# A hybrid decoder layer on one Trainium2 core: the down-projection's 22 blocks in seven products, with the weight sums made in DRAM

## The chip, the cores and the metric

The kernel runs on one core of one Trainium2 chip. A core has a matrix engine (TensorE, in the profile PE; its weight loads are PEld) that multiplies a 128 x 128 weight tile with up to 512 columns and adds into banks of PSUM, a vector engine (VectorE, DVE), an activation engine (ScalarE, ACT), GpSimd (POOL) and a queue engine (SyncE, SP) that issues DMAs. ACT and POOL issue DMAs too; a DMA that adds to its destination is issued by POOL here. The metric is device time in microseconds, the median of three runs.

## The reference

One layer on x of 1024 tokens by 1024 channels, in float32. Only its last part matters here:

```python
def conv_ffn(xn, w_up, conv_w, conv_b, w_down):
    u = xn @ w_up                                # 1024 -> 2 x 2816
    upad = jnp.pad(u, ((0, 0), (CONV_WIDTH - 1, 0), (0, 0)))
    c = conv_b
    for j in range(CONV_WIDTH):                  # causal, width 3
        c = c + upad[:, j:j + S] * conv_w[j]
    gate, val = jnp.split(c, 2, axis=-1)
    return (jax.nn.silu(gate) * val) @ w_down    # 2816 -> 1024
...
    x = x + conv_ffn(xn, w_up[l], conv_w[l], conv_b[l], w_down[l])
return rmsnorm(x, norm_final_w)
```

Ahead of it lie a norm, the input projection, two attentions, gates and a mixing projection with a residual sum.

## The kernel before

Everything lies with channels on the 128 partitions and tokens along the row. Each float32 operand is split in two parts that sum to it: a high part (a cast by ACT) and a low part (a subtraction by DVE). A product of two blocks is three matmuls: high by high, weight-high by activation-low, weight-low by activation-high. A matmul needs the weight tile and the activation tile in parts, so DVE and ACT prepare both while PE works.

**Up-projection** (`hidden`, from line 922; its matmuls are line 919). It runs over 22 pairs j of output blocks (gate j, value j). A pair is a 2 x 2 block product done with seven products in place of eight; sums of weights are made by POOL (`sum_pair`, lines 121 to 124), sums of the seven results by DVE (`recombine`, lines 478 to 485, reading PSUM). Seven products of four blocks are 84 matmuls of 512 columns. Then POOL multiplies with the norm factor (line 1063), ACT and DVE apply the convolution (lines 1072 to 1075), DVE multiplies gate and value (1056), and SP stores the hidden block h_j to DRAM (`hd`). `next_w` keeps one pair of weights ahead; the weights' loads (`raw`, `rv`) are in SP's queue.

**Down-projection** (`down`, from line 1078). Output blocks m = 0 to 7, token halves 0 and 1, 22 hidden blocks.

- The first N1 = 6 hidden blocks are multiplied plainly: 16 pieces of three blocks, each for both halves (line 1120), so 288 matmuls; each output tile is added into `x3`, the residual, by DVE (line 1147).
- The other 16 blocks form a 2 x 2 problem (left and right eight blocks, upper and lower four outputs) in seven products P1, P5, P6, P3, P7, P2, P4, each over 4 outputs m and 8 blocks: 24 matmuls per step (line 1169). Products that share terms go on adding in the same PSUM bank ("chains": banks "y" for P1, P6, P7, P4 and "d" for P5, P3, P2), and after each DVE adds the bank into one or two tiles of `x3` (line 1176). A stage's activations are sums of h blocks (`operand`, DVE lines 1034 to 1045) that are then split (`parts_h`, lines 838 and 839). A stage's weights are sums too: four tiles `S` in SBUF are loaded by SP, negated by ACT (line 108) and added to by POOL's DMA (`add_to`, line 91) between stages.
- Step by step the program calls `next_w`, the product, loads of later h blocks (`fetch`), two `prep` calls (one operand each), and the evictions owed from the step before.
- The convolution of the last pair is deferred into the first pieces (`DEFER`), its stores likewise (`STORE`).
- P4's last two outputs are done in two halves of 256 columns, so that the final norm of the first quarter (`last_norm`: column sums on PE, a power on POOL, a spread on PE, scaling by DVE and POOL, stores) overlaps the last matmuls.

The compiler's tile layer orders each engine's instructions from the program's order and its own estimates; `issue_after` puts an instruction behind a given one on the same engine.

## Time and profile before

| | |
|---|---|
| median of three runs | 1330.38 us (1330.3 to 1331.21) |
| the profiled execution | 1330.42 us, its span 1328.4 us |
| granted TensorE clock | 0.998 |
| matmuls in the span | 6264 |
| up-projection, first pair to last | about 674.9 to 1097.3 us of the span |
| down-projection, plain part (line 1120) | 1097.3 to 1162.6 us |
| down-projection, seven products (line 1169) | 1162.6 to 1318.8 us |
| final norm and stores after the last matmul | 1318.8 to 1328.4 us |

Times within the span are counted from its first instruction. A "busy" engine is one with an instruction under way; for PE the ends are modelled, so the pace is read from starts or from the chain of waits, not from the mean of one matmul (which overlaps the next).

### The profile page before, as it was taken

How to read it: one execution, taken by the hardware profiler on the slowest of the kernel's cores; microseconds unless marked ns; L12 is line 12 of the kernel's file. 1: busy time of each engine (PE TensorE's matmuls, PEld its weight loads, DVE VectorE, ACT ScalarE, POOL GpSimd, SP SyncE). 2: the span in 40 equal slices, each digit the busy share in tenths (PEclk: the TensorE clock that was granted, in tenths of full speed). 3: DMA queues.
4: the chain of work that ended last, by engine and by line, in shares of the span. 5: the costliest groups of instructions: out<-in, count | busy, mean ns of one | idle time of the engine just before them, and what ended most of it. 6: DMA issues, size and time to landing. Idle time of an engine off the chain costs nothing.

```text
span 1328.4 us, 17040 instructions
## 1 busy us (share of the span) xinstructions
PE 1315.8 (99%) x6264; PEld 1097.6 (83%) x6264; DVE 1049.4 (79%) x1431; ACT 614.7 (46%) x946; POOL 478.0 (36%) x364
## 2 busy tenths in 40 slices
PE   9999999999999999999999999999999999999997
PEld 7888888888888878888888888888888888888886
DVE  8846775289888976455669999999999997886654
ACT  9432232276667774333444443343434344345643
POOL 0446652001101015751435666665566631101111
PEclk9999999999999999999999999999999999999999
DMA  7334333966554236334422222122222228867532
GB/s 260 126 144 157 145 148 122 269 179 190 143 133 142 82 126 225 120 118 151 143 95 95 80 79 93 66 95 80 82 77 86 81 75 333 266 158 143 111 98 108
DMA packets 63234, 180.25 MB, mean 136 GB/s; under 512 B 6960, under 2 KB 16816, under 8 KB 63152
## 3 DMA queue, kind: packets, MB, share of 16 engines
q1 hardware_dynamic: 49120, 153.48, 35.1%
q0 software_dynamic: 2304, 8.39, 3.7%
q10 hardware_dynamic: 11728, 17.31, 3.6%
q8 instruction: 49, 0.80, 0.3%
q14 instruction: 33, 0.27, 0.1%
HBM read 130.39 MB, written 48.76 MB: 135 GB/s over the span
## 4 chain that ended last, share of the span: by engine, by line
PE 97%; ACT 1%; DVE 1%; DMA 0%; issue 0%; SPq 0%; POOLq 0%; POOL 0%; ACTq 0%
PE t L919 45%; PE y L1169 7%; PE d L1169 5%; PE g L177 4%; PE g L178 4%; PE g L179 4%; PE sc L177 3%; PE sc L179 3%; PE sc L178 3%; PE sc L651 3%; PE y L1120 2%; PE d L1120 2%; PE t L667 1%; PE t L770 1%; PE sc L739 1%; PE t L679 1%
## 5 line engine op out<-in xcount | busy, mean ns | idle before, releaser
L1063 POOL TENSOR_TENSOR us<-us,rstd 128x1024 f32<-128x1024 f32 x42 | 92.2, 2214 | 82.5 <-DVE us L484 47.6
L1072 ACT ACTIVATE c<-us,vecs 128x1024 f32<-128x1024 f32 x44 | 54.8, 1248 | 127.1 <-POOL us L1063 121.5
L137 DVE TENSOR_TENSOR sl<-sf,sh 128x1024 fp32r<-128x1024 f32 x62 | 89.3, 1441 | 12.8 <-ACT sh L135 12.8
L158 DVE TENSOR_TENSOR wl<-raw,wh 128x1024 fp32r<-128x1024 f32 (+1 forms) x49 | 68.0, 1389 | 35.5 <-ACT wh L156 25.9
L135 ACT CAST sh<-sf 128x1024 fp32r<-128x1024 f32 x62 | 64.6, 1044 | 62.1 <-PE t L919 44.0
L156 ACT CAST wh<-raw 128x1024 fp32r<-128x1024 f32 (+1 forms) x49 | 49.6, 1014 | 91.2 <-PE sc L178 33.4
L121 POOL TENSOR_TENSOR sf<-rv 128x512 f32<-128x512 f32 x30 | 50.4, 1679 | 99.5 <-DVE sl L137 59.0
L1169 PE MATMUL y<-h,wh 128*128 128x512 f32 (+1 forms) x288 | 80.8, 366 | 0.0
L1075 DVE SCALAR_TENSOR_TENSOR c<-us,vecs,c 128x1024 f32<-128x1024 f32 x44 | 78.5, 1817 | 0.0
L1074 DVE SCALAR_TENSOR_TENSOR c<-us,vecs,c 128x1024 f32<-128x1024 f32 x44 | 69.3, 1606 | 5.6 <-ACT c L1072 5.5
L123 POOL TENSOR_TENSOR sf<-raw,rv 128x512 f32<-128x512 f32 x30 | 56.7, 1890 | 46.6 <-DVE sl L137 46.6
L177 PE MATMUL g<-xh,wh 128*128 128x512 f32 x176 | 71.0, 404 | 1.5 <-ACT g L580 1.5
L178 PE MATMUL g<-xl,wh 128*128 128x512 f32 x176 | 70.3, 400 | 0.0
L179 PE MATMUL g<-xh,wl 128*128 128x512 f32 x176 | 70.2, 399 | 0.0
L1055 ACT ACTIVATE c<-c 128x1024 f32<-128x1024 f32 x22 | 23.4, 1063 | 83.4 <-DVE c L1075 83.4
L655 DVE CUSTOM_DVE_ANT_0 L<-sc,bias 128x128 f32<-128x128 f32 (+7 forms) x64 | 47.7, 752 | 17.0 <-PE sc L651 13.7
L634 POOL MEMSET aT<- 128x128 f32 x32 | 6.1, 204 | 151.8 <-PE t L680 98.0
L137 DVE TENSOR_TENSOR wl<-raw,wh 128x1024 fp32r<-128x1024 f32 (+1 forms) x32 | 59.7, 1864 | 0.1
L1169 PE MATMUL d<-h,wh 128*128 128x512 f32 x192 | 59.4, 390 | 0.0
L1169 PEld LDWEIGHTS y<-h,wh 128*128 128x128 f32 x288 | 52.1, 189 | 8.7
L122 POOL TENSOR_TENSOR sf<-sf,raw 128x512 f32<-128x512 f32 x31 | 58.2, 1878 | 2.2
L656 ACT ACTIVATE L<-L,sm 128x128 f32<-128x128 f32 (+7 forms) x64 | 49.6, 778 | 20.0 <-DVE sm L655 17.3
(411 smaller groups left out, 4255.4 us busy)
## 6 DMA issues: line engine op xcount, KB each, us to landing
u<-qd SPq DMA_DIRECT2D x72, 256.0 KB, 6.4
raw<-in_w_up SPq DMA_DIRECT2D x23, 512.0 KB, 3.5
raw<-in_w_in SPq DMA_DIRECT2D x22, 512.0 KB, 3.7
hd<-c SPq DMA_DIRECT2D x22, 512.0 KB, 2.6
rv<-in_w_up SPq DMA_DIRECT2D x21, 512.0 KB, 3.6
gr<-gd SPq DMA_DIRECT2D x16, 512.0 KB, 3.4
S<-in_w_down POOLq DMA_DIRECT2D x16, 512.0 KB, 6.7
qd<-us SPq DMA_DIRECT2D x15, 512.0 KB, 2.6
```

Source lines behind the costliest of these rows:

```text
L122: tt(sa[:, 1], sa[:, 0], g[:, 0], ALU.subtract)
L135: cast = nc.scalar.copy(hi, src)
L137: low = nc.vector.tensor_tensor(lo, src, hi.bitcast(F32), ALU.subtract)
L158: self.lo = (eng or nc.vector).tensor_tensor(wl, raw, wh.bitcast(F32), ALU.subtract)
L177: nc.tensor.matmul(ps, wh[:, kc + o, :], ah, start=first and n == 0, stop=False)
L178: nc.tensor.matmul(ps, wh[:, kc + o, :], al, start=False, stop=False)
L179: nc.tensor.matmul(ps, wl[:, kc + o, :], ah, start=False, stop=last and n == len(kcs) - 1)
L919: nc.tensor.matmul(ps, (ah, ah, al)[p][:, k, :], (bh, bl, bh)[p], start=first and n == p == 0, stop=last and p == 2 and n == len(ks) - 1, ...
L1063: i = (nc.vector if m % NF == 0 else nc.gpsimd).tensor_tensor(us[:, 2:], us[:, 2:], self.rstd, ALU.mult)
L1074: nc.vector.scalar_tensor_tensor(c, us[:, 1:T + 1], cw[1], c, ALU.mult, ALU.add)
L1075: nc.vector.scalar_tensor_tensor(c, us[:, 0:T], cw[0], c, ALU.mult, ALU.add)
L1169: nc.tensor.matmul(ps, v[:, k, :], x, start=start and k == i == 0, stop=k == 7 and i == 2, skip_group_check=True)
```

## The change

All 22 hidden blocks go into the seven products (11 left, 11 right), and the plain part is gone. Each stage is cut in two steps per output, over blocks 0 to 5 and 6 to 10 (`CUTS`), so 18 and 15 matmuls a step. The order is P1, P2, P5, P6, P3, P7, P4. Signs move to the activations and evictions (`operand`, `evict`), so the weight sums are additions alone. They are made in DRAM tensors `sd` by `sums_of`: 16 copies issued by SP and 16 adding DMAs issued by POOL, each 128 rows of 1408 floats (704 KB), two steps per pair from pair 1 of the up-projection on, behind that pair's last weight load on SP (`self.sync`) and last weight sum on POOL (`self.sum`). The weights are then loaded like any other. The `S` tiles, their negation and additions in the down-projection go. P4 is split in columns only in its second cut. The scaling pieces of the first quarter are called among those of the last one, DVE's behind its last eviction.

```diff
-HP, HPB, HR = 11, 9, 8
-STORE = (1,9)
-DEFER = (4,8)
-N1 = 6
+HP, HPB, HR = 6, 14, 11
+STORE = (1, 6)
+DEFER = (2, 5)
+HK = NF // 2
+CUTS = ((0, 6), (6, 11))
-STAGES = ("P1", "P5", "P6", "P3", "P7", "P2", "P4")
+STAGES = ("P1", "P2", "P5", "P6", "P3", "P7", "P4")
...
-        if self.deep and self.wsrc and len(self.wsrc[0]) == 2 and not isinstance(self.wsrc[0][1], str):
-            src, nk = self.wsrc[0]
-            self.wsrc[0] = src, nk, None, None, self.load_raw(src, nk)
+        for i in range(min(2, len(self.wsrc)) if self.deep else 0):
+            if len(self.wsrc[i]) == 2:
+                self.wsrc[i] += None, None, self.load_raw(*self.wsrc[i])
...
+    def sums_of(self):
+        nc, d = self.nc, self.sd
+        row = lambda m, r: self.w_dn[m].rearrange("p k c -> p (k c)")[:, r * HK * P:(r + 1) * HK * P]
+        copy = lambda n, src: lambda m: nc.sync.dma_start(d[n][m], src(m))
+        add = lambda n, o, r: lambda m: nc.gpsimd.dma_start(d[n][m], row(m + o, r), accum_op=ALU.add)
+        for step in (copy("P5", lambda m: row(m + 4, 0)), copy("P7", lambda m: row(m + 4, 0)), add("P5", 4, 1), add("P7", 0, 0),
+                     copy("P6", lambda m: d["P5"][m]), add("P6", 0, 0), copy("P3", lambda m: d["P6"][m]), add("P3", 0, 1)):
+            for m in range(4):
+                step(m)
+                yield
...
+                    for _ in range(2 if j else 0):
+                        with tc.issue_after(self.sync), tc.issue_after(self.sum):
+                            next(sums, None)
...
         elif stage == "P6":
-            tt(a, a, R["B22", k], ALU.subtract)
+            self.nc.vector.scalar_tensor_tensor(a, a, -1.0, R["B22", k], ALU.mult, ALU.subtract)
...
-            def product(ps, w, stage, start, a=0, b=H2, each=None):
-                for k in range(8):
+            def product(ps, w, stage, c, start, a=0, b=H2, each=None):
+                k0, k1 = CUTS[c]
+                for k in range(k0, k1):
...
+            count = {0: 3, 1: 2, 3: 1, 6: 3, 7: 2}
+            chains, owed, tail, i = [{}, {}], [], [], 0
+            for stage in STAGES:
+                which, start, o, hf, done = plan[stage]
+                for c in range(2):
+                    for m in range(4):
+                        if stage == "P4" and c == 1 and m > 1:
+                            break
...
+                        product(ps, w, stage, c, start)
...
+                        prep(count.get(i, 0) if i < 8 else 2 if i % 4 < 2 or i < 16 else 1)
...
+                        if c:
+                            owed = [lambda ps=ps, m=m + o, hf=hf, done=done: evict(ps, m, hf, done)]
...
+                        i += 1
...
-                    product(ps, w, "P4", False, a, b, lambda k, m=m: tail.pop(0)() if a and k == (4 if m < 3 else 2) else None)
+                    product(ps, w, "P4", 1, False, a, b, each)
...
+                if a:
+                    def held(f):
+                        with tc.issue_after(ev.ins):
+                            f()
+                    last[1:1] = [lambda f=f: held(f) for f in tail[2:]]
+                    last[:0] = [lambda f=f: held(f) for f in tail[:2]]
```

## The prediction

> **What bounds the kernel now.** I read the page first, then the chain of waits in order of time, then the windows.

> ```profile
> PE 1315.8 (99%) x6264; PEld 1097.6 (83%) x6264; DVE 1049.4 (79%) x1431; ACT 614.7 (46%) x946; POOL 478.0 (36%) x364
> DVE  8846775289888976455669999999999997886654
> PEclk9999999999999999999999999999999999999999
> ```
> ```profile
> 702.10 395.23 PE t L919 x1740
> 1097.32 2.04 PE d L1120 x9
> ...
> 1160.56 2.04 PE y L1120 x9
> 1162.60 21.76 PE y L1169 x96
> ...
> 1316.95 1.80 PE y L1169 x15
> ```
> ```profile
> 930.00:968.00 38.00, 38.00 (x169) 31.23 (x168) 37.72 (x33) 15.64 (x18) 23.95 (x16) 1.00 0.25 84
> 1140.00:1160.00 20.00, 20.00 (x90) 16.57 (x89) 17.44 (x26) 7.30 (x13) 2.84 (x3) 1.00 0.83 254
> ...
> sum 200.00, PE 200.00 PEld 165.86 DVE 144.44 ACT 95.47 POOL 24.50; mean PE 20.00 PEld 16.59 DVE 14.44 ACT 9.55 POOL 2.45
> ```

> PE is busy 99%, at the full granted clock, and from 702.10 to 1318.76 the chain is matmul after matmul. The pace is 21.76 / 96 = 0.2267 us for a matmul of 512 columns (2.04 / 9 in the plain part, the same) and 1.80 / 15 = 0.12 us for one of 256. So a matmul that goes away in the down-projection is worth its pace, as long as the other engines keep up.

> The window rows (after the stretch: its length, then busy PE, PEld, DVE, ACT, POOL) are of different stages. The first, 38 us of the up-projection, has DVE at 37.72: there, DVE has no room either. The last sums ten windows of 20 us from 1100 to 1300, the down-projection, the middle row its fullest one: DVE 144 of 200, POOL 24.5. The change puts less on PE in the roomy stage, and new work on POOL and the DMA engines in the tight one.

> **The matmuls.** Before, counted from the code: 288 plain ones, and 7 x 4 x 24 = 672, of which P4's last two outputs (48) run as 96 of 256 columns. That is 912 full and 96 half. After: 7 x 4 x 33 = 924, of which the second cut of P4's last two outputs (2 x 15) runs as 60 halves: 894 full and 60 half. Gone are 18 x 0.2267 = 4.08 and 36 x 0.12 = 4.32, together **8.4 us**. Nothing hides this: the chain runs through these matmuls.

> **DVE, ACT and PSUM in the down-projection.**

> ```profile
> L158 DVE TENSOR_TENSOR wl<-S,wh 128x1024 fp32r<-128x1024 f32 x16 | 19.6, 1224 | 2.1 <-ACT wh L156 2.1
> L158 DVE TENSOR_TENSOR wl<-raw,wh 128x768 fp32r<-128x768 f32 x7 | 6.7, 956 | 3.3 <-ACT wh L156 3.2
> L839 DVE TENSOR_TENSOR h<-ha,h 128x512 fp32r<-128x512 f32 x32 | 20.8, 689 | 2.1 <-ACT h L838 2.1
> L1041 DVE TENSOR_TENSOR hb<-hc,hb 128x512 f32<-128x512 f32 x8 | 5.8, 733 | 1.7 <-DMA hc<-hd 1.6
> L1147 DVE TENSOR_TENSOR x<-x,d 128x512 f32<-128x512 f32 x8 | 5.5, 683 | 0.0
> L156 ACT CAST wh<-raw 128x768 fp32r<-128x768 f32 x7 | 5.8, 828 | 9.7 <-PE y L1120 7.3 <-issue 2.4
> ```

> Weight tiles: 8 x 0.956 + 28 x 1.224 = 41.9 before. After, 28 of six blocks (0.956) and 28 of five (no row; between 0.956 for six and 0.689 for four, I take 0.82) are 49.7: +7.8. Operand splits go from 62 to 71: 9 x 0.689 = +6.2. Operand sums go from 32 to 44: 12 x 0.69 to 0.73, +8.5 (the fused form that replaces some is an estimate at the same length). Evictions lose the plain part's 16: -10.9. DVE gains 11.6 us and stands near 156 of some 192 us, 81%. The average leaves room; the bursts are what to look at.

> With a step number i (eight per stage), the program puts eight operands into steps 12 to 15, all of stage P5's with a sum: 8 x 1.38 = 11.0, weights 3 x 0.82 + 0.96 = 3.4, three evictions with norms 4.1: 18.5 us against 60 matmuls, 13.6 us. Steps 8 to 11 before it have 12.0 us against 72 x 0.2267 = 16.3. Together 30.5 against 29.9. Two things ease it: these operands are first needed at step 16, and DVE's instructions overlap:

> ```profile
> 1147.84 2.50 DVE L839 TENSOR_TENSOR h<-ha,h 128x512 fp32r<-128x512 f32 x4
> ```

> Four in 2.50 is 0.62 each, a tenth under the mean of one, which makes 27.5 of 29.9. What would hurt PE is a weight tile split late. A tile's buffer comes free a step ahead, so in a step of 15 matmuls (3.40 us), after the cast (0.828 at most) and the split (0.82), DVE may be 1.75 us late. I take 0.6 us for the whole stage; the bounds are 0 (it runs ahead in steps 8 to 11) and 3.5, worked out under the rivals. ACT had 95 of 200 and loses the negations; POOL loses the adds here. The new operands wait for h loads as the old ones do, and PSUM is no tighter: one chain set of four banks starts where the plain part filled eight at once.

> **The sums in DRAM, on SP, POOL and the DMA engines.**

> ```profile
> L91 POOL DMA_DIRECT2D S<-in_w_down x16: 856/866/1105, 1153.8 to 1247.5; - x16
> S<-in_w_down POOLq DMA_DIRECT2D x16, 512.0 KB, 6.7
> q0 software_dynamic: 2304, 8.39, 3.7%
> q1 hardware_dynamic: 49120, 153.48, 35.1%
> 1153.83 1.98 POOL L91 DMA_DIRECT2D S<-in_w_down  x2 [17.04 <-DMA S<-in_w_down]
> rv<-in_w_up SPq DMA_DIRECT2D x21, 512.0 KB, 3.6
> ```
> ```profile
> 951.48 0.68 DVE L480 TENSOR_TENSOR u<-t,s 128x512 f32<-128x512 f32 x1
> 952.25 0.45 PE L919 MATMUL t<-T_0h,sh 128*128 128x512 f32 x1
> 952.54 0.39 PE L919 MATMUL t<-T_0l,sh 128*128 128x512 f32 x1
> 953.91 0.10 POOL L1062 MEMSET us<- 128x2 f32 x1
> 956.09 4.40 POOL L1063 TENSOR_TENSOR us<-us,rstd 128x1024 f32<-128x1024 f32 x2 [2.08 <-DVE us L484]
> 956.51 2.12 DVE L137 TENSOR_TENSOR wl<-rv,wh 128x512 fp32r<-128x512 f32 x1
> 960.52 1.25 ACT L1072 ACTIVATE c<-us,vecs 128x1024 f32<-128x1024 f32 x1 [1.15 <-POOL us L1063]
> 961.49 2.47 DVE L1074 SCALAR_TENSOR_TENSOR c<-us,vecs,c 128x1024 f32<-128x1024 f32 x2
> ```
> ```profile
> POOL sf L123 <- DVE sl L137: 39.8, 18, 2.3
> POOL us L1063 <- DVE us L484: 37.4, 18, 2.1
> POOL sf L121 <- DMA rv<-in_w_up: 36.7, 17, 3.4
> PEld t L919 <- DVE u L480: 1.6, 7, 0.2
> ```

> Thirty-two steps, two per pair from pair 1, end at pair 16. Pairs 1 to 4, 9, 10, 13 and 14 have copies alone, issued by SP behind that pair's loads. Each add or copy that needs an earlier step needs one issued four to six pairs ago, so no engine waits there. Eight pairs (5 to 8, 11, 12, 15, 16) have two adds each on POOL.

> An add behind POOL's last sum falls into the gap of 2.08 us before line 1063, where POOL waits for DVE. The old adds held POOL for 0.866 us; they have 128 rows too, longer ones now. Two are 1.73 us: inside the gap. If the issue grew with the bytes (704 / 512), two would be 2.4, and line 1063 would start 0.3 late. Behind it wait ACT's two convolutions, then DVE; the second ends at 961.77, and DVE's second instruction on line 1074 begins near 962.7 (half of 2.47 on), so about 1 us more is free. Past that, DVE is late, and PE with it: PE's weight load waits for line 480 in 7 of 18 pairs, because that frees the bank of the next product (it ended at 952.16; PE's matmul of 952.25 took 0.45, the next one 0.39). The up-projection has a pair in 84 x 395.23 / 1740 = 19.08 us, against 19.04 from the pace: a microsecond that DVE loses there stays lost, and the most that a lucky shift could win over all pairs is 22 x 0.04 = 0.8.

> The adds' transfers: 3.7% of 1328 us over 16 is 3.07 us of all engines per 512 KB, so 4.2 per 704 KB, two in a pair of 19.1 us are 0.44 on top of the window's 0.25. There is room on average. The load `rv` would land later beside them; POOL's next sums wait for it, and behind them POOL waits 2.2 us for DVE anyway (line 123), so that much is free.

> [...]

> I take +0.3 us for the up-projection, with bounds -0.8 and +23.

> **The tail.**

> ```profile
> 1317.44 1.84 POOL L1259 TENSOR_TENSOR x<-x,rstd 128x768 f32<-128x768 f32 x1 [2.21 <-ACT rstd L1251]
> 1318.78 0.43 DVE x L1223
> 1320.88 0.70 POOL rs L194
> ```

> From the last matmul (1318.76) to the end are 9.6 us. The last two halves now hold 30 matmuls of 0.12 instead of 48, so the first quarter's scaling (POOL 1.84) no longer ends inside them: it begins about as the last matmul ends, holds POOL near the 2.1 us at which the last power wants it, and its stores crowd those of the last quarter. I take +0.4, bounds -0.3 and +1.8 (all of the 1.84).

> **Sum.** -8.4 + 0.6 + 0.3 + 0.4 = -7.1 us. The profiled execution took 1330.42 (its span of 1328.4 and 2.0 around it, which I leave as they are); the median of the runs is 1330.38, so nothing is corrected. **Forecast 1323.3 us.** With all low bounds 1330.4 - 8.4 - 0.8 - 0.3 = 1320.9.

> **Rivals.**

> *The bursts starve PE.* If operands don't run ahead, steps 12 to 15 are 18.5 - 13.6 - 1.75 = 3.1 us late, and stage P3's second cut (six operands of 1.38, 3.4, 4.1: 15.8 against 13.6) 0.4 more. That is 2.9 more than I took: 1326.2. For it: DVE is at 17.4 of 20 already in places of this stage. Against: PE never waited there, and loads of h run steps ahead.

> [...]

> *More than forecast.* POOL and DVE disturb each other: `wl<-rv` took 2.12 against 0.69 for the same form in the down-projection, while line 1063 ran. If line 1063 comes a little later, DVE may go first; PE's pace caps that at 0.8 us: 1321.

> [...]

> **How the numbers follow.** The forecast with its terms moved within their bounds (1321 to 1325.5) has 0.66; the bursts (to 1328) 0.14; the adds 0.16, of which the mild half of a third ends near no change; more than forecast 0.04. About 0.2% (2.7 us) is what a measurement can tell from none. Faster than 1327.7: 0.66 + 0.04 + most of the bursts and a little of the adds, 0.78; within: 0.08; slower: 0.14. The range 1320.4 to 1332 leaves out the bad end of the adds and little else; the likeliest case alone is 1321 to 1325.5.

> **What would show it.** Line 1169's matmuls: 924 in place of 960 by pace, and none of line 1120. In the chain, whether matmuls still follow one another after the up-projection, with gaps at steps 12 to 17 if bursts bite. In the up-projection, POOL's issue of one add against 0.87, and the pair's length against 19.08 in pairs 5 to 8: this decides between forecast and slower. The time from the last matmul to the end against 9.6. I am wrong if a pair with adds takes over 20 us, or if PE waits for weights over 3 us in all.

## The result, and the profile after

The changed kernel is slower: 1336.09 us median of 6 runs (1334.9 to 1337.98) against 1330.62 for the kernel before on the same chip (6 runs, 1330.3 to 1331.21), a ratio of 1.0041, 95% interval 1.0028 to 1.0054. The profiled execution took 1335.52 us, its span 1333.7. Forecast were 1323.3 and a range of 1320.4 to 1332.

The page of the changed kernel, busy time and instructions by engine:

```profile
PE 1312.1 (98%) x6210; PEld 1090.0 (82%) x6210; DVE 1056.9 (79%) x1456; ACT 621.2 (47%) x967; POOL 479.5 (36%) x364
```

The matmuls are gone as counted: 6264 before, 6210 after, 54 fewer, where 288 + 672 + 48 became 924 + 30. So the work left, and the time did not. PE's timeline says where it stayed; a bracket is idle time just before a row, and what ended it.

```profile
1097.88 0.62 PE L1112 MATMUL y<-sh,wh 128*128 128x512 f32 x2
...
1103.41 0.73 PE L1112 MATMUL y<-sh,wh 128*128 128x512 f32 x2 [1.30 <-ACT wh L139]
1105.48 0.51 PE L1112 MATMUL y<-sh,wl 128*128 128x512 f32 x1 [1.34 <-DVE wl L141]
...
1109.02 0.39 PE L1112 MATMUL y<-sl,wl 128*128 128x512 f32 x1
1112.02 0.73 PE L1112 MATMUL y<-sh,wh 128*128 128x512 f32 x2 [2.61 <-ACT wh L139]
...
1132.27 0.61 PE L1112 MATMUL y<-h,wh 128*128 128x512 f32 x2
1135.62 0.80 PE L1112 MATMUL y<-h,wl 128*128 128x512 f32 x1 [2.74 <-DVE wl L141]
1136.21 1.06 PE L1112 MATMUL y<-h,wh 128*128 128x512 f32 x2
...
1140.90 0.73 PE L1112 MATMUL d<-h,wh 128*128 128x512 f32 x2 [0.24 <-ACT wh L139]
```

Every one of these waits is for the cast (`wh`) or the split (`wl`) of a weight tile, and all lie in the first 43 us of the down-projection. After 1140.90 the timeline has no bracket until the tail. The waits of the stretch from 1095 to 1145 (total, times, longest):

```profile
PEld y L1112 <- DVE wl L141: 7.0, 5, 3.2
...
PE y L1112 <- DVE wl L141: 4.8, 4, 2.7
...
PE y L1112 <- ACT wh L139: 3.9, 2, 2.6
```

The difference can be laid out by the starts of matmuls. "Up" is from the up-projection's first `t<-T_0h,wl` to the first matmul of the down-projection, "down" from there to the start of the last one, "idle" the brackets of PE in "down".

| profiled execution | up | down | idle | time |
|---|---|---|---|---|
| before | 403.80 | 221.30 | 0 | 1330.42 |
| after | 404.62 | 225.69 | 9.00 | 1335.52 |

Down should have been 221.3 - 8.4 = 212.9. It is 12.8 us more, of which 9.0 are gaps. The other 3.8 are what follows a gap: two matmuls of 1136.21 took 0.86 to the next row, 0.43 each in place of 0.2267, and this pace held from 1135.62 to 1138.35; after the shorter gaps one matmul took 0.34. Up is 0.8 longer, and from the last matmul's start to the span's end it is 10.1 after 9.9 before. -8.4 + 12.8 + 0.8 + 0.2 = +5.4, and the spans differ by 5.3.

**What makes the tiles late.** First four rows of the kernel before, from the timelines of ACT, DVE and PE:

```profile
1102.28 0.81 ACT L156 CAST wh<-raw 128x768 fp32r<-128x768 f32 x1
...
1104.20 0.95 DVE L158 TENSOR_TENSOR wl<-raw,wh 128x768 fp32r<-128x768 f32 x1
...
1105.32 0.62 PE L1120 MATMUL d<-sh,wh 128*128 128x512 f32 x2
1105.78 0.39 PE L1120 MATMUL d<-sh,wl 128*128 128x512 f32 x1
```

This is the second weight tile. PE came to it at 1105.32. Its split ended at 1105.15, and the first matmul that takes the split (`wl`) began at 1105.78, 0.63 us later. So the tile was just as late before; nobody saw it, because the first one lasted 36 matmuls, both halves of the columns, 8.16 us from 1097.16. In the changed kernel the second tile:

```profile
1101.40 1.24 ACT L1056 ACTIVATE c<-us,vecs 128x1024 f32<-128x1024 f32 x1 [3.26 <-POOL us L1047]
1102.55 0.81 ACT L139 CAST wh<-raw 128x768 fp32r<-128x768 f32 x1
...
1104.47 0.95 DVE L141 TENSOR_TENSOR wl<-raw,wh 128x768 fp32r<-128x768 f32 x1
```

Cast and split end within 0.3 us of where they did before. But a tile now serves one half, 18 matmuls, 4.08 us, and PE wants it at 1101.96. In front of the cast stands a deferred convolution that waits 3.26 us for POOL. The next tiles follow from the chain of waits of the changed kernel (start, length, what):

```profile
1104.56 0.88 DVE wl L141
...
1105.45 0.34 SPq L129
...
1107.74 6.41 DMA ha<-hd
...
1114.17 0.04 ACT h L820
...
1114.70 0.84 ACT wh L139
...
1115.56 0.97 DVE wl L141
...
1116.60 2.01 POOL us L1047
...
1118.63 1.25 ACT c L1056
...
1119.91 0.06 DVE c L1058
...
1121.11 0.83 DVE wl L141
...
1121.98 2.86 PE y L1112 x12
```

Read it as a queue: the late split of the second tile (1104.56) frees the buffer for which the next weight load (L129) waits on SP, the loads of `h` stand behind that load, one of them takes 6.41 us to land, ACT's cast of that operand waits for it, the weight's cast stands behind that in ACT's order, its split behind it, POOL's multiplication for a convolution behind the split, the convolution behind POOL, the next split behind the convolution, and PE at the end. Before, this chain was matmul after matmul here, and the first loads of `h` for the later operands went out 7.4 us earlier. First the kernel before, then the changed one:

```profile
1098.46 1.44 SPq L1012 DMA_DIRECT2D hb<-hd  x3
```
```profile
1105.85 2.32 SPq L999 DMA_DIRECT2D ha<-hd  x5
```

The longest gap, 2.74 us at 1135.62, lies after the chain shown. The cast of that tile had ended at 1131.00, but its split began 3.75 us later, behind an operand's sum that waited for a load of `h`, an eviction and a convolution in DVE's order:

```profile
1131.65 1.39 DVE L1020 TENSOR_TENSOR ha<-ha,hb 128x512 f32<-128x512 f32 x2 [4.62 <-DMA hb<-hd]
...
1134.75 0.82 DVE L141 TENSOR_TENSOR wl<-raw,wh 128x640 fp32r<-128x640 f32 x1
```

### The profile page after: what moved, and what is told of

Read it like the earlier page. It is cut to its first block, busy times and chain, and to the rows that moved or that the text cites. A ratio compares the mean times of both kernels' runs of the same rounds, so it can differ in the third digit from the quotient of the medians.

```text
span 1333.7 us, 17123 instructions
## 1 busy us (share of the span) xinstructions
PE 1312.1 (98%) x6210; PEld 1090.0 (82%) x6210; DVE 1056.9 (79%) x1456; ACT 621.2 (47%) x967; POOL 479.5 (36%) x364
## 3 DMA queue, kind: packets, MB, share of 16 engines
q0 software_dynamic: 2304, 11.54, 4.5%
## 4 chain that ended last, share of the span: by engine, by line
PE 82%; DVE 7%; issue 4%; DMA 2%; POOL 2%; ACT 2%; SPq 0%; POOLq 0%; DVEq 0%; ACTq 0%
PE t L901 32%; PE y L1112 7%; PE d L1112 7%; PE g L160 4%; PE g L161 4%; PE g L162 4%; PE sc L161 3%; PE sc L162 3%; PE sc L160 3%; PE sc L633 3%; DVE wl L120 1%; DVE c L1058 1%; PE t L649 1%; DVE c L1059 1%; PE t L752 1%
## 5 line engine op out<-in xcount | busy, mean ns | idle before, releaser
L141 DVE TENSOR_TENSOR wl<-raw,wh 128x1024 fp32r<-128x1024 f32 (+2 forms) x85 | 97.3, 1145 | 52.7 <-ACT wh L139 43.0
L139 ACT CAST wh<-raw 128x1024 fp32r<-128x1024 f32 (+2 forms) x85 | 74.1, 873 | 130.2 <-PE y L1112 53.5
L120 DVE TENSOR_TENSOR sl<-sf,sh 128x1024 fp32r<-128x1024 f32 x62 | 95.9, 1548 | 14.7 <-ACT sh L118 14.7
L177 POOL TENSOR_TENSOR rs<-ms,mhalf 128x8 f32<-128x8 f32 (+2 forms) x9 | 13.3, 1474 | 235.8 <-DVE ms L175 229.7
L1112 PE MATMUL y<-h,wh 128*128 128x512 f32 (+1 forms) x324 | 96.1, 380 | 0.0
L1112 PE MATMUL d<-h,wh 128*128 128x512 f32 x264 | 81.3, 389 | 0.2 <-ACT wh L139 0.2
L1059 DVE SCALAR_TENSOR_TENSOR c<-us,vecs,c 128x1024 f32<-128x1024 f32 x44 | 74.4, 1724 | 0.0
L1112 PEld LDWEIGHTS y<-h,wh 128*128 128x128 f32 x324 | 60.1, 190 | 11.3
L1058 DVE SCALAR_TENSOR_TENSOR c<-us,vecs,c 128x1024 f32<-128x1024 f32 x44 | 64.3, 1490 | 4.1 <-ACT c L1056 3.9
L1112 PE MATMUL y<-h,wl 128*128 128x512 f32 (+1 forms) x162 | 61.9, 382 | 3.3 <-DVE wl L141 3.2
L120 DVE TENSOR_TENSOR wl<-raw,wh 128x1024 fp32r<-128x1024 f32 (+1 forms) x32 | 62.8, 1962 | 0.1
L638 ACT ACTIVATE L<-L,sm 128x128 f32<-128x128 f32 (+7 forms) x64 | 49.6, 778 | 19.9 <-DVE sm L637 17.3
## 6 DMA issues: line engine op xcount, KB each, us to landing
raw<-in_w_up SPq DMA_DIRECT2D x23, 512.0 KB, 4.9
raw<-in_w_in SPq DMA_DIRECT2D x22, 512.0 KB, 3.8
hd<-c SPq DMA_DIRECT2D x22, 512.0 KB, 2.6
rv<-in_w_up SPq DMA_DIRECT2D x21, 512.0 KB, 4.6
gr<-gd SPq DMA_DIRECT2D x16, 512.0 KB, 3.4
```

What stands on the lines that cost most here:

```text
L120: low = nc.vector.tensor_tensor(lo, src, hi.bitcast(F32), ALU.subtract)
L139: self.hi = nc.scalar.copy(wh, raw)
L141: self.lo = (eng or nc.vector).tensor_tensor(wl, raw, wh.bitcast(F32), ALU.subtract)
L1058: nc.vector.scalar_tensor_tensor(c, us[:, 1:T + 1], cw[1], c, ALU.mult, ALU.add)
L1059: nc.vector.scalar_tensor_tensor(c, us[:, 0:T], cw[0], c, ALU.mult, ALU.add)
L1112: nc.tensor.matmul(ps, v[:, k - k0, :], x, start=start and k == i == 0, stop=k == HK - 1 and i == 2, skip_group_check=True)
```

## The experiments

The theories have letters in the expectations. Q: the short tiles lost the cover that hid late casts and splits, which stand in ACT's and DVE's queues behind convolutions and operands that wait for POOL or for loads. A: the additions in DRAM cause it. D: the DMA engines are too full there, whatever the order. U: two additions in one pair lengthen the up-projection. Where one run is given, its time has no interval, and the changed kernel's own runs spread over 3 us; the traces carry those comparisons.

**Loads of h first** (an order of SP alone):

```diff
+            with tc.high_priority(300):
+                for n in range(2):
+                    fetch(*loads[n][0])
             for stage in STAGES:
...
-                        if i < 2:
-                            fetch(*loads[i][0])
```

> Only SP's order changes: the five loads of hidden blocks 6 to 10 are issued ahead of the fifth weight load, which waits for a buffer. Theory Q (weight tiles that now last 4.1 or 3.4 us sit in ACT's and DVE's queues behind instructions that wait for something else): the loads land about 5 us earlier, ACT no longer holds the third tile's cast behind their casts, PE's gap of 2.61 + 0.26 us near 1112 goes and with it some slow restart: 3 to 4 us less than the changed kernel, 1332 to 1333; the gaps near 1103, 1105 and 1135 stay. Theory D (the DMA engines are too crowded there, the loads land late whatever their order): nothing changes, about 1336.

Measured: 1335.69 us in one run; down 223.31, idle 7.99, up 406.72. The gap of 2.61 us at the third tile shrank to 1.22, as the `h` casts no longer waited so long (0.82 us at the longest for the first ones, 5.78 in the changed kernel), but gaps of 1.69 and 1.33 at the second tile and of 2.58 at 1135.77 stayed. The expected gain of 3 to 4 us did not come: down is 2.4 us shorter, up 2.1 longer. Late loads are one of the things ahead of the weights, not all of them.

**No deferred convolutions.** The last three convolutions, with their products and so rows 20 and 21 of `h`, are left out.

> The three deferred convolutions of the last pairs are left out (the blocks are stored as they come from the up-projection), everything else stays. Theory Q: POOL's multiplication and ACT's convolution no longer stand ahead of the weight casts, so the gaps of 1.30, 1.34 and 0.51 us near 1103, 1105 and 1122 go: 3 to 5 us less than the changed kernel, 1331 to 1333, while the gap near 1112 (late loads) stays. Theory D: under 1 us of change.

```diff
-                        self.defer.append(f)
+                        self.defer.append(lambda after=None, j=j, w=w, us=us: self.late.append(lambda: nc.sync.dma_start(self.hd[j], us[w][:, 2:])) if w else None)
```

Measured: 1330.68 in one run; down 219.15, idle 3.39. PE's longest gaps in the timeline of this kernel:

```profile
1105.04 0.50 PE L1112 MATMUL y<-sh,wl 128*128 128x512 f32 x1 [0.59 <-DVE wl L141]
...
1110.38 0.73 PE L1112 MATMUL y<-sh,wh 128*128 128x512 f32 x2 [1.42 <-ACT wh L139]
```

With the convolutions out, 5.6 of 9.0 us of gaps went, and down fell by 6.5. The gap at 1135 is gone altogether. The edit also takes work off ACT, DVE and POOL, so this run alone does not tell the order of the work from its amount.

**The kernel before with short tiles.** Nothing of the change but its tile size: the plain part's eight weight tiles of six blocks become sixteen of three, each for 18 matmuls.

```diff
-        src += [(self.w_dn[m:m + 2, :, n * c:n * c + n, :].rearrange("m p k c -> p m k c"), 2 * n) for m, c in self.pieces[::2]]
+        src += [(self.w_dn[m, :, n * c:n * c + n, :], n) for m, c in self.pieces]
```

> The kernel before, with the plain part's weights loaded and split in 16 tiles of three blocks in place of 8 of six: a tile lasts 18 matmuls, 4.1 us, as in the changed kernel, with the same bytes and the same matmuls. Theory Q: PE waits for weights in the first 25 us of the down-projection, 2 to 6 us in all, 1332 to 1337. Theory D, and the theory that the adds did it: no gaps, 1330.4 within 1 us.

Measured: 1340.87 in one run, 9.8 us over the kernel before beside it (1331.05); down 230.57 for 221.30, idle 5.45. Its timeline:

```profile
1103.15 0.73 PE L1118 MATMUL d<-sh,wh 128*128 128x512 f32 x2 [1.05 <-ACT wh L156]
1104.55 0.50 PE L1118 MATMUL d<-sh,wl 128*128 128x512 f32 x1 [0.66 <-DVE wl L158]
...
1117.93 0.73 PE L1118 MATMUL d<-h,wh 128*128 128x512 f32 x2 [1.29 <-ACT wh L156]
...
1130.32 0.50 PE L1118 MATMUL d<-h,wl 128*128 128x512 f32 x1 [2.45 <-DVE wl L158]
```

Gaps of the same kind in the same stretch, with neither new products nor sums in DRAM. Here 9.3 us are lost, 5.45 of them in gaps. So shorter tiles are enough to uncover the lateness, which is the core of Q. They do it in more than one way, and this run does not part them: the first gap lies at a cast about as late as before (1102.61 after 1102.28), the one at 1117.93 behind casts of `h` whose loads SP issued only at 1104.91, as in the changed kernel behind a weight load that waits for a buffer, and the one at 1130.32 behind a deferred convolution in DVE's order.

**No sums.** Copies and additions are left out, and the four stages that use sums read plain quarters of the weight.

> The copies and adds in DRAM are left out and the stages take plain quarters of the weights; all else stays. The up-projection should win back its 0.7 us. Theory Q and theory D: the gaps of the first 45 us of the down-projection stay, 1335 within 1. Theory A (the adds delay the up-projection's end, and the lateness is carried into the down-projection): gaps go too, 1324 within 2.

```diff
-                    for _ in range(2 if j else 0):
-                        with tc.issue_after(self.sync), tc.issue_after(self.sum):
-                            next(sums, None)
```

Measured: 1336.53 in one run, half a microsecond over the expected range; up 403.90, down 226.35, idle 6.73, with gaps of 1.73, 1.33 and 2.86 us where the changed kernel has them. Without the additions up is 0.7 us shorter than in the changed kernel's trace, and the down-projection loses as much; A falls.

**Another order at the border**, same arithmetic: the loads of `h` first, as above; the first two weight tiles ahead of the last convolution in the up-projection; POOL's multiplications apart from their convolutions, and early; in steps 0 to 15 everything else of a step behind its weight's cast and split.

```diff
...
+                        hi, lo = self.whi, self.wlo
+                        with ExitStack() as edges:
+                            if i < 16:
+                                edges.enter_context(tc.issue_after(hi.ins))
+                                edges.enter_context(tc.issue_after(lo.ins))
+                            if i in DEFER:
+                                self.defer.pop(0)(lo)
+                            prep(count.get(i, 0) if i < 8 else 2 if i % 4 < 2 else 1)
+                        if i in (0, 1):
+                            self.mults.pop(0)(lo)
...
```

> The changed kernel with the same arithmetic, and another order of the work around the start of its down-projection: the first two weight tiles are cast and split before the last deferred convolution's ScalarE part, the multiplications of the deferred convolutions run on GpSimd early, convolutions and operands of steps 0 to 15 are placed behind that step's weight cast and split, five loads of h go to SP ahead of the weights. Theory Q (a weight tile now serves 15 to 18 matmuls, and its cast and split stand in ScalarE's and VectorE's queues behind work that waits for GpSimd or for loads): PE's gaps in the first 45 us fall from 9.0 to under 3 us, the down-projection from first to last matmul from 225.7 to under 217, the time 1324 to 1329, faster than before. Theory D (the DMA engines are too full at the start of the down-projection, whatever the order): the gaps stay at 6 us or more, the time at 1332 to 1337.

Measured: 1332.03 median of 10 runs, ratio to before 1.0008 (0.9999 to 1.0018); down 221.26, idle 4.60. Half of the gaps went, and 4 us of the time. Both expectations missed: Q's (gaps under 3 us, down under 217, 1324 to 1329), and D's on the gaps (6 us or more), while the time lies at the edge of D's range. Against D: the same bytes in another order, and down is 4.4 us shorter; the next version settles it. One large gap was left, 3.39 us at 1113.65, at the third tile: three operands of step 0 stood ahead of its cast and split, waiting 6.45 us for `ha`.

**The order carried further**: no operand in step 0, the convolutions in steps 3, 5 and 6 in place of 0, 3 and 4.

```diff
-DEFER = (0, 3, 4)
+DEFER = (3, 5, 6)
...
-            count = {0: 3, 1: 2, 3: 1, 6: 3, 7: 2}
+            count = {1: 2, 2: 2, 3: 1, 4: 1, 5: 1, 6: 2, 7: 2}
```

> The version with another order at the start of the down-projection, with that order carried further: no operand is made in step 0, so the cast and split of the third weight tile stand ahead of everything that waits for the loads of h; the deferred convolutions move from steps 0, 3, 4 to 3, 5, 6, with the stores, loads and GpSimd multiplications that go with them. Theory Q (the rest of the gaps, 4.6 us, is the third tile's cast and split behind h casts that wait for their loads and a convolution that GpSimd slowed): gaps in the first 45 us under 1.5 us, down-projection 217 to 218.5 us from first to last matmul, time 1326 to 1329. Theory V (VectorE has too much to do in the first 16 us, 19.9 of 20 busy, whatever the order): the gaps move and stay at 3 us or more, 1330 to 1333.

Measured: 1328.87 in one run; down 217.05, idle 2.14 where under 1.5 was expected, the largest gap 0.75. Neither the DMA engines nor DVE's load was the limit (D and V fall). Up was 406.21 here, 2.4 us over the kernel before, from two pairs of 20.0 us, 0.8 to 0.9 over their neighbours.

**Additions one per pair, pairs 5 to 20**, in the changed kernel alone, and with the order above.

> The changed kernel with one edit: the sixteen additions in DRAM are issued one per pair in pairs 5 to 20, in place of two per pair in eight pairs; the copies move with them. The arithmetic is the same. Theory U (two additions in one pair crowd the loads of that pair, which made the up-projection 0.7 to 3.7 us longer than that of the kernel before, by run): the up-projection's pairs stay at 19.04 to 19.2 us, down-projection starts within 0.7 us of before's 1097.2, and the time falls by 1 to 2 us from 1336 to about 1334.5. Rival (what makes the up-projection longer is something else, such as the DVE queue): pairs of 19.4 to 20 us stay, 1336.

> Both edits together: additions one per pair, and the order at the start of the down-projection carried further. If theories Q and U both hold: 1324 to 1327.5 us, below the kernel before by 0.25 to 0.5%. If only Q holds: 1326 to 1329. If only U holds: 1329 to 1332.

Measured: 1340.68 median of 4 (ratio 1.0075, 1.0058 to 1.0091) and 1332.46 of 10 (1.0010, 1.0001 to 1.0020). Both expectations missed, and the traces say how: no pair from the second to the twentieth is over 19.27 us, so U was right on them, yet up is 410.51 and 410.46. All of it lies in the next one, 22.7 us where that pair has 16.3 otherwise, here in the timeline of the version with both edits:

```profile
1069.37 1.66 POOL L87 DMA_DIRECT2D sdP<-in_w_down  x2
...
1070.93 0.99 SPq L975 DMA_DIRECT2D sf<-hd  x2
...
1080.02 0.62 ACT L824 CAST rv<-sf 128x512 fp32r<-128x512 f32 x1 [14.75 <-DMA sf<-hd]
...
1081.02 1.05 ACT L121 CAST wh<-raw 128x1024 fp32r<-128x1024 f32 x1
...
1082.12 0.80 PE L905 MATMUL t<-B_0h,wh 128*128 128x512 f32 x1 [3.27 <-ACT wh L121]
```

The last two additions were issued together. Two loads of `h`, issued 1.6 us behind them, released ACT 8.1 us after their issue ended; the up-projection's last weight cast stood behind them, and PE waited 3.27 us and then took 0.43 us for a matmul from 1082.71 to 1087.83, with a granted clock of 0.50 in the window from 1082 to 1086 (1.00 in the same window of the version with the order alone). In the version with the order alone (additions done by pair 16) the same cast began 2.4 us after that issue.

**The same, pairs 2 to 17.**

```diff
+        at = {"P5": ((1, 2, 2, 3), (3, 4, 5, 6)), "P7": ((1, 4, 9, 14), (2, 7, 16, 17)),
+              "P6": ((5, 6, 7, 8), (8, 9, 10, 11)), "P3": ((10, 11, 12, 13), (12, 13, 14, 15))}
```

(For each sum: the pairs in which its four copies are issued, and its four additions.)

> The changed kernel with only the schedule of the additions changed (one per pair, in pairs 2 to 17); the order at the start of the down-projection is that of the changed kernel. Theory Q: the up-projection is as long as before, the down-projection still loses 9 us of gaps or a little under, 1333.5 to 1335.5, slower than before by 0.2 to 0.4%. If the additions were behind the gaps too: below 1330.

> The version with both edits, the additions one per pair again, but in pairs 2 to 17 in place of 5 to 20. In the version with pairs 5 to 20 the pairs without a neighbour addition stayed at 19.04 to 19.2 us, and all of the loss, 6.5 us, stood in pair 20: the last two additions were issued together at 1069.4, the h loads issued at 1070.9 behind them came 14.7 us late to ScalarE, and its weight cast stood behind them. Theory U2 (an addition in DRAM that meets loads delays them; alone in a pair with room it costs nothing): the down-projection starts within 0.7 us of 1097.2, lasts 215.4 to 217, and the time is 1324 to 1326.5, 0.3 to 0.5% below the kernel before. Rival U3 (the order at the border itself delays the end of the up-projection, whatever the additions): start at 1100 or later, 1328 to 1332.

With this schedule alone: 1335.22 median of 6 (ratio 1.0030, 1.0018 to 1.0042); up 403.92, down 225.99, idle 6.34. With the order at the border too: **1327.25 us, median of 9 runs (1326.31 to 1328.5), against 1331.01; ratio 0.9973, interval 0.9964 to 0.9983.** This version is faster than both kernels; time and down lie just outside the expected ranges (1324 to 1326.5 and 215.4 to 217). Against the version beside it, which has the same additions, the order alone is worth 8.0 us. Its waits and windows (length, busy PE, PEld, DVE, ACT, POOL, granted clock, DMA share, GB/s):

```profile
PE y L1128 <- DVE wl L148: 1.0, 2, 0.7
...
PE d L1128 <- DVE h L829: 0.8, 1, 0.8
```
```profile
1100.00:1110.00 10.00, 9.34 (x40) 7.17 (x40) 8.14 (x13) 3.44 (x6) 0.00 (x0) 1.00 0.96 345
1110.00:1120.00 10.00, 10.00 (x46) 8.26 (x45) 9.64 (x10) 5.09 (x7) 2.59 (x2) 1.00 1.04 400
```

Up is 403.97, as long as before; down 217.57, 3.7 less than before; 2.31 us of gaps are left, and down is still 4.7 over the 212.9 that the matmuls need. The same stretch of the changed kernel:

```profile
1100.00:1110.00 10.00, 6.78 (x28) 4.64 (x26) 7.10 (x9) 2.58 (x3) 1.36 (x1) 1.00 0.63 207
1110.00:1120.00 10.00, 7.72 (x33) 6.09 (x34) 7.71 (x9) 5.94 (x9) 2.00 (x1) 1.00 0.94 304
```

DVE does more in the better version's 20 us (17.78 against 14.81), and the DMA engines move more (345 and 400 GB/s against 207 and 304): neither was the limit, only the order of what they did.

| kernel | up | down | idle |
|---|---|---|---|
| loads of h first | 406.72 | 223.31 | 7.99 |
| no deferred convolutions | 406.09 | 219.15 | 3.39 |
| before, short tiles | 403.89 | 230.57 | 5.45 |
| no sums | 403.90 | 226.35 | 6.73 |
| other order | 405.74 | 221.26 | 4.60 |
| order carried further | 406.21 | 217.05 | 2.14 |
| additions in pairs 5 to 20 | 410.51 | 223.67 | 5.65 |
| both | 410.46 | 215.39 | 1.18 |
| additions in pairs 2 to 17 | 403.92 | 225.99 | 6.34 |
| these and the order | 403.97 | 217.57 | 2.31 |

## Why the prediction was wrong

**Matmuls, -8.4:** right. The count fell as worked out, the pace is unchanged (from 1200.59 the chain has 132 matmuls in 29.92 us, 0.2267 each), and the best version shows 3.7 us of the gain; its gaps and what follows them still take the other 4.7.

**DVE, ACT and PSUM in the down-projection, +0.6 within 0 and 3.5:** this step failed; it was 12.8. Of the ten windows of 20 us from 1100 to 1300 after, one of the two fullest of DVE, and the sum:

```profile
1160.00:1180.00 20.00, 20.00 (x90) 16.56 (x89) 20.00 (x33) 14.88 (x24) 0.00 (x0) 1.00 0.87 301
...
sum 200.00, PE 190.95 PEld 155.53 DVE 148.63 ACT 100.04 POOL 5.79; mean PE 19.10 PEld 15.55 DVE 14.86 ACT 10.00 POOL 0.58
```

The sum of DVE's work was nearly right (148.6 for "near 156"), and so was the sentence that the average leaves room. Two sentences were wrong. "The new operands wait for h loads as the old ones do": they wait longer (ACT's first such wait is 5.78 us, 3.67 before), as SP issued the loads later; and a weight's cast queued behind them had 8.16 us of matmuls to hide it, and now has 4.08. And "a tile's buffer comes free a step ahead ... DVE may be 1.75 us late" priced only a tile's own cast and split, with nothing before them in the queue. The bound of 3.5 came from the bursts at steps 12 to 15, and there no gap appeared: counted in matmuls from 1140.90, these steps lie at about 1157 to 1170, and the window from 1160 has DVE busy for 20.00 of 20 us and PE too. A full DVE starved nobody; a DVE and an ACT with room (13.63 and 8.19 us busy of the 20 from 1120), but with waits in their queues, did. I had looked where most instructions are added, not where the removed stage had covered something. The rows of the kernel before in the section on the result, a margin of 0.63 us, were there to be read.

**The sums in DRAM, +0.3 within -0.8 and 23:** 0.8 in the changed kernel's trace; 1.9 to 2.9 in the four other versions with two additions per pair, all of them with another edit too. With one per pair, early, it is 0.1 to 0.2. That the changed kernel's runs spread over 3 us is not explained by this: those of the version with early additions alone spread as far (1334.14 to 1337.53). Lines of the changed kernel on the additions:

```profile
L87 POOL DMA_DIRECT2D sdP<-in_w_down x16: 803/1056/1138, 800.5 to 1012.9; - x16
```
```profile
sdP<-in_w_down POOLq DMA_DIRECT2D x16, 704.0 KB, 9.2
rv<-in_w_up SPq DMA_DIRECT2D x21, 512.0 KB, 4.6
```

The issue took 1.06 us in the median for the 0.87 taken, so two fill the gap of 2.08 on POOL. `rv` landed in 4.6 us, 1.0 later than before, inside the 2.2 that were free. No run shows the upper bound of 23, nor an addition that holds POOL long enough for it: the longest issue in the changed kernel took 1.14 us, and the longest up of any version is 410.51, 6.7 over the kernel before.

**The tail, +0.4:** measured +0.2.

**The rivals:** the chance of 0.16 for the adds was on the right side and for the wrong place; they would have shown as pairs over 20 us, and the longest with additions is 19.42 in the changed kernel (up to 20.05 in other versions with two per pair). *The bursts* had one of the two engines and the wrong steps, and about a quarter of the size. The line "I am wrong if PE waits for weights over 3 us in all" named the symptom: 4.8 + 3.9 us.

## What to carry to other kernels

Where a change removes a stage or shortens the time that one tile serves, look at what that stage was hiding: take each instruction that the next consumer needs, find when it ended in the old trace and when the new schedule will want it, and read what stands ahead of it in its engine's queue. An average of 80% said nothing about this; the margin here was 0.63 us. Look at SP's queue too: here a weight load that waited for a buffer stood ahead of loads of `h`, which went out 7.4 us later than before. Then order the queues so that what feeds the bounding engine stands ahead of anything that waits for loads or for other engines.

## What the runs showed of the hardware

```profile
1135.00:1145.00 10.00, 9.14 (x33) 7.16 (x34) 10.00 (x15) 3.59 (x7) 0.00 (x0) 0.83 0.84 290
```

The length of one gap does not decide it here. In the version without sums a matmul took 0.43 us from 1106.96 to 1112.08, right after gaps of 1.73 and 1.33 us with two matmuls between them; with the additions in pairs 2 to 17 alone it was 0.43 from 1108.16 to 1113.28, after gaps of 1.70 and 1.33. With the loads of `h` first it took 0.23 from 1136.10 to 1138.85, after one of 2.58. What decides was not tried. What followed the gaps cost up to as much as the gaps did: in the changed kernel 6 matmuls at 0.43 in place of 0.2267 made 1.2 us, but without sums down is 13.45 us over the 212.9, and only 6.73 of them are gaps.

**Loads behind additions in DRAM.** Alone in a pair, in pairs 2 to 17, the additions cost the up-projection 0.1 to 0.2 us in all (403.92 and 403.97 against 403.80). Where two were issued at once, 1.6 us ahead of two loads of 256 KB, the loads released their reader only 8.1 us after issue, at least 5.7 later than in the version without additions there (8.1 against at most 2.4). For `rv`, 512 KB, it was 1.0 (4.6 us in the changed kernel for 3.6 before). What set the 5.7 was not tried.
